# Weights split in pieces of 1024 columns, and a pair's products in another order

## The chip, the cores and the metric

One core of one Trainium2 chip runs the whole program. The metric is the device time of one execution in microseconds. The kernel before takes 1662.88 us (median of three runs, 1662.47 to 1663.27).

## The reference

One inference step of a backbone of one layer for 128 context tokens and 512 latent tokens (640 rows, width 1024): an FFN half step (SwiGLU, inner width 2816), a mixer (a chunkwise mLSTM in both directions beside a gated convolution, merged by gates and projected), a second FFN half step, and a last RMS norm. Each norm is modulated by vectors computed from the condition (adaLN). Cut to what matters here:

```
h = modulate(rmsnorm(x, norm_g[0]), sh1, sc1)
x = x + 0.5 * g1 * swiglu(h, ffn1_w1, ffn1_w2)
h = modulate(rmsnorm(x, norm_g[1]), shm, scm)
z = h @ w_in + b_in            # q, k, v, o, gates, convolution inputs
ml = (o * mlstm(q, k, v, ...)) @ w_ml_out
sc = (bg * conv3(cg * xs)) @ w_sc_out
x = x + gm * ((sigmoid(z_gml) * ml + sigmoid(z_gsc) * sc) @ w_o)
h = modulate(rmsnorm(x, norm_g[2]), sh2, sc2)
x = x + 0.5 * g2 * swiglu(h, ffn2_w1, ffn2_w2)
```

All of it is float32. Nearly all the work is the products of the weights with 640 columns of activations.

## The kernel before

The activations lie transposed, 128 features by 640 tokens, in two halves of 320 columns. A weight block of 128 output features and 1024 inputs is loaded as one tile of 128x1024 (`wr`, five buffers, DMAs on SP's queue).

To reach float32 accuracy with float32r products each operand is split in two: `split` (L74) lets ACT round the tile to float32r (L75, `wh`) and DVE subtract that from the raw tile (L79, `wl`). `three` (L242) then issues three products of 128x128 weights by 320 columns (L245 to L247: high by high, high by low, low by high). A piece of weights that is split at once is here called an op: 512 columns before, so two for a tile; six `wh` and six `wl` buffers, and splitting runs up to four ops ahead (OPB, AHEAD, L82). `cast_more` (L102) issues the splits, in the order in which the ops are used, when an earlier op is taken up by `op()`. `hold` and `release` keep the ops of a stage in their buffers for its second half.

Most of the large products go by pairs (`pair_el`, `pair_steps`, L260): two output blocks against both halves of the columns, as a Strassen-Winograd scheme with seven products instead of eight. A11, A12, A21 and A22 are the quarters of the two weight tiles. S1 = A21 + A22, S2 = S1 - A11, S3 = A11 - A21 and S4 = A12 - S2 are summed on DVE (L218; in ten pairs of the mixer S1 and S3 on POOL). The matching sums of activations (T1 to T4) are ready beforehand. Each of the seven products is four k-blocks by three, so 12 products of 320 columns in a PSUM bank. Partial results are shared between the banks: a gets A11, and ACT copies it into b; b gets S2, and ACT copies that into c (both L273 and L283); b gets S4, c gets S3 and A22, and a gets A12. S1 goes into a bank of its own, which ACT copies out (L279, `p5`).

There are 72 pairs: 38 in the two FFNs, 34 in the mixer. Before, the products stand in the order A11, S1, S2, A12, S3, S4, A22. Each engine works through its own instructions in the order in which the program issues them, with semaphores between engines; there is no scheduler behind it. In each pair other work is woven in: the SwiGLU of the pair before (silu, product, split of `Uh`/`Ul`), sums for the adaLN vectors on DVE (L696), the steps of the mLSTM.

Other stages are plain: `plain_el` (one weight tile by both halves; the second FFN matrix, w_ml_out, w_sc_out, w_o), `halves_el` (the last output blocks before a norm, first all with the first half of the columns, then all with the second, so that the norm can begin), and `head_el` (the first three blocks behind a norm, while the normalised activations are still being split). `first_head` is that for the start of the kernel, where weights, adaLN and activations arrive together; in it nine products of a zero bfloat16 tile (L1110) are issued ahead of the first real ones.

Of the kernel before, what the change touches and what calls it, by code (L numbers as in the profile page):

```python
# [12 lines left out]
P = 128  # L13
# [31 lines left out]
def mixer_step(ctx: ExitStack, tc: tile.TileContext, x_prompt, x_sample, state_C, state_n, state_m,  # L45
# [36 lines left out]
    RAWB, OPB, SB, AHEAD = 5, 6, 4, 4  # L82
    raws, ops = [], []
# [18 lines left out]
    def cast_more(upto):  # L102
        load_more()
        while ptr["cast"] < min(upto, ptr["held"] + OPB, ptr["cap"], len(ops)):
            n = ptr["cast"]
            if not ready(ops[n]):
                return
            while ptr["sum"] < min(n + 2, len(ops)) and ready(ops[ptr["sum"]]):
                o = ops[ptr["sum"]]
                o["ap"] = o["src"](o)  # L110
                ptr["sum"] += 1
            o = ops[n]
            w = o["n"]
# [5 lines left out]
            rdone.update(o["last"])  # L119
            load_more()  # L120
# [87 lines left out]

    LH, RH = slice(0, 512), slice(512, 1024)

    def pair_ops(r1=0, r2=1, e1=None):
        e1 = e1 or V

        def total(key, engine, fn, a, b):
            def src(o):
                g = o["group"].setdefault(r1, {})
                t = g[key] = ring.tile([P, 512], F32, name="ws", bufs=SB)
                getattr(engine, fn)(t, part(o, a), part(o, b))  # L218
                return t
            return src  # L220

        def part(o, key):
            if key[0] == "S":
                return o["group"][r1][key]
            return rtile[o["base"] + (r1 if key[1] == "1" else r2)][:, LH if key[2] == "1" else RH]

        whole = lambda key: lambda o: part(o, key)
        spec = lambda src, *r: {"raws": list(r), "n": 512, "src": src}
        return {
            "A11": spec(whole("A11"), r1), "A12": spec(whole("A12"), r1), "A22": spec(whole("A22"), r2),  # L230
            "S1": spec(total("S1", e1, "tensor_add", "A21", "A22"), r2),
            "S2": spec(total("S2", V, "tensor_sub", "S1", "A11"), r1, r2),
            "S3": spec(total("S3", e1, "tensor_sub", "A11", "A21"), r1, r2),
            "S4": spec(total("S4", V, "tensor_sub", "A12", "S2"), r1, r2),
        }
# [3 lines left out]
    EARLY = ("A11", "A12", "S1", "S2", "S3", "S4", "A22")  # L239
# [20 lines left out]
    def pair_steps(order, ev, spare_v):  # L260
        S = {}

        def prod(name, ps, start):
            hi, lo = op()
            for kk in range(4):
                three(ps[:, :HT], hi, lo, kk, HB[ACT_OF[name]][kk], start and kk == 0, kk == 3)

        for name in order:
            if name == "A11":
# [4 lines left out]
                flush()  # L274
            elif name == "S1":
# [4 lines left out]
            elif name == "S2":  # L280
                prod(name, S["b"], False)
                S["c"] = big()
                A.copy(S["c"][:, :HT], S["b"][:, :HT])  # L283
            elif name == "A12":
                prod(name, S["a"], False)
                ev(0, 0, S["a"][:, :HT])
# [18 lines left out]
    def pair_el(load1, load2, ev, e1=None, spare_v=False):  # L305
        po = pair_ops(e1=e1)

        def emit():
            nf = len(fill)
            for i, _ in enumerate(pair_steps(ORDER, ev, spare_v)):  # L310
                relax(7 - i if i else 9)
                drain(nf - nf * (i + 1) // 7)
        return dict(element([load1, load2], [po[name] for name in ORDER], emit), pair=True)

    def tile_ops(nk, t=0):
        out = []
        for k0 in range(0, nk, 4):
            n = min(4, nk - k0) * P
            out.append({"raws": [0], "n": n,
                        "src": (lambda k0, n: lambda o: rtile[o["base"] + t][:, k0 * P:k0 * P + n])(k0, n)})  # L320
        return out

    def unit(w, nk, acts, h, ev, points=()):
        ps = big()
        for k in range(nk):
            three(ps[:, :HT], *w[k // 4], k % 4, acts(k, h), k == 0, k == nk - 1)
# [9 lines left out]
    def head_el(blocks, chain, work, mid=(), extra=None):  # L336
# [7 lines left out]
        def emit():  # L344
# [20 lines left out]
            w = [[op()] for t in range(3)]  # L365
            ps = [big() for t in range(3)]
            for k in range(KT):
                if k == 4:
                    for t in range(3):
                        w[t].append(op())  # L370
                for t in range(3):
                    three(ps[t][:, :HT], *w[t][k // 4], k % 4, plain_acts(k, 0), k == 0, k == KT - 1)
# [12 lines left out]
            for t in range(3):  # L385
                unit(w[t], KT, plain_acts, 1, ev(t), {3: some, 7: some})
                release(2)
            if extra:
                extra()
            for t in range(3, nb):  # L390
                w = [op(), op()]
# [8 lines left out]
        oa = [dict(tile_ops(KT, at_[t])[i], raws=[at_[t]]) for i in range(2) for t in range(3)]  # L400
        ob = [dict(o, raws=[at_[t]]) for t in range(3, nb) for o in tile_ops(KT, at_[t])]
        el = dict(element(loads, oa + ob, emit), calm=True)
# [5 lines left out]
    def halves_el(loads, nk, acts, ev, after):  # L408

        per = (nk + 3) // 4  # L410

        def emit():
# [4 lines left out]
            for m in range(len(loads)):  # L417
                w = [op() for _ in range(per)]
                ws.append(w)
                unit(w, nk, acts, 0, lambda h, ps, m=m: ev(m, h, ps))  # L420
                squares()
                after(0, m)
            n = 6 // len(loads)
# [5 lines left out]
            for m in range(len(loads)):  # L429
                pts = {nk // 2 - 1: nxt} if n == 2 else {}  # L430

                def done(h, ps, m=m):
# [3 lines left out]
                    else:  # L436
                        ev(m, h, ps)
                        release(per)
                        if m == len(loads) - 1 or n == 2:
# [5 lines left out]
                unit(ws[m], nk, acts, 1, done, pts)  # L445
                if m < 2:
                    release(per)
                    squares()
        return element(loads, [dict(o, raws=[t]) for t in range(len(loads)) for o in tile_ops(nk, t)], emit)

    def plain_el(load, nk, acts, ev, halves=(0, 1)):
        def emit():
            nf = len(fill)
            ps = {h: big() for h in halves}
            w = [op() for _ in range(0, nk, 4)]
            n = 0
            for k in range(nk):
                hi, lo = w[k // 4]
                for h in halves:
                    three(ps[h][:, :HT], hi, lo, k % 4, acts(k, h), k == 0, k == nk - 1)  # L460
                relax(nk - k)
                drain(nf - nf * (k + 1) // nk)
            for h in halves:
                ev(h, ps[h][:, :HT])
            squares()
        return dict(element([load], tile_ops(nk), emit), calm=True)
# [484 lines left out]
    def ffn(w1, w2, g, lists, head_of, e1=None):  # L951

        head, els, f0 = [], [], 0
        for size in GROUPS:
            U = {}
            grp = []
            for j in range(size):
# [17 lines left out]
                else:  # L975
# [4 lines left out]
            w2s = [plain_el(ld(m), size, acts, lambda h, ps, m=m, last=last: add_x(m, h, ps, g, last))  # L980
                   for m in range(KT if not last else 2)]
            w2s[0] = dict(w2s[0], calm=False)
            if last:
                w2s.append(halves_el([ld(m) for m in range(2, KT)], size, acts,
                                     lambda m, h, ps: add_x(m + 2, h, ps, g, True), lists))
# [23 lines left out]
    early = early_x.enter_context(pool("early", side="right"))  # L1009
    for k in range(KT):  # L1010
# [5 lines left out]
    def x_load(ch):  # L1016

        for q in range(2):
            t = XI[ch, q] = ring.tile([P, 512], F32, name=("wh", "wl")[q], bufs=OPB)
# [53 lines left out]
    def first_head(blocks):  # L1073
# [17 lines left out]
        part = lambda t, c: {"raws": [t], "n": 512, "src": lambda o: rtile[o["base"] + t][:, c:c + 512]}  # L1091
# [932 lines left out]
```

## Time and profile before

| | before |
|---|---|
| median of 3 runs | 1662.88 us |
| span of the profiled execution | 1659.7 us |
| TensorE matmul busy | 1642.4 us, 99% |
| TensorE weight load busy | 1601.4 us, 96% |
| DVE busy | 1257.6 us, 76% |
| ACT busy | 791.5 us, 48% |
| POOL busy | 170.7 us, 10% |
| products of `three` (L245 to L247) | 10080 |

The page gives the span of the profiled execution, from its first to its last instruction; no separate time is listed for it. The median of the runs is 3.2 us above it. Products overlap in the array, so the duration of one (0.31 us) is longer than the distance to the next (0.146 us), and it is the distance that counts. A row of a timeline gives start, duration, engine, line, operation, the tile written and the tiles read; in brackets, how long the engine was idle before and on whom it waited.

### The profile page before, as it was taken

How to read it: one execution, taken by the hardware profiler on the slowest of the kernel's cores; microseconds unless marked ns; L12 is line 12 of the kernel's file. 1: busy time of each engine (PE TensorE's matmuls, PEld its weight loads, DVE VectorE, ACT ScalarE, POOL GpSimd, SP SyncE). 2: the span in 40 equal slices, each digit the busy share in tenths (PEclk: the TensorE clock that was granted, in tenths of full speed). 3: DMA queues.
4: the chain of work that ended last, by engine and by line, in shares of the span. 5: the costliest groups of instructions: out<-in, count | busy, mean ns of one | idle time of the engine just before them, and what ended most of it. 6: DMA issues, size and time to landing. Idle time of an engine off the chain costs nothing.

```text
span 1659.7 us, 29315 instructions
## 1 busy us (share of the span) xinstructions
PE 1642.4 (99%) x11201; PEld 1601.4 (96%) x11201; DVE 1257.6 (76%) x2681; ACT 791.5 (48%) x1723; POOL 170.7 (10%) x258
## 2 busy tenths in 40 slices
PE   8999999999999999999999999999999999999998
PEld 5999999999999999999999999999999999999997
DVE  6867877877778878778897898789587467476576
ACT  5642542533566656555561455532375245254253
POOL 2010000000031322111121221011100000000002
PEclk9999999999999999999999999999999999999999
DMA  9454333343352434342367323366241322232222
GB/s 321 115 165 127 111 111 111 102 136 101 108 178 80 113 88 111 75 109 67 96 208 239 106 79 92 101 196 207 90 127 55 99 77 79 74 93 87 77 77 64
DMA packets 273036, 193.08 MB, mean 116 GB/s; under 512 B 7923, under 2 KB 253050, under 8 KB 272896
## 3 DMA queue, kind: packets, MB, share of 16 engines
q1 hardware_dynamic: 263280, 158.36, 32.5%
q0 software_dynamic: 9584, 32.85, 6.8%
q8 instruction: 88, 1.44, 0.4%
q14 instruction: 52, 0.43, 0.1%
q10 hardware_dynamic: 32, 0.01, 0.0%
HBM read 175.87 MB, written 15.31 MB: 115 GB/s over the span
## 4 chain that ended last, share of the span: by engine, by line
PE 91%; DVE 3%; ACT 3%; DMA 2%; issue 1%; SPq 1%; POOL 0%; ACTq 0%; DVEq 0%; POOLq 0%
PE ps L245 28%; PE ps L246 28%; PE ps L247 28%; PE ax L1583 2%; PE ax L1614 2%; DMA wr<-in_ffn_w_dram 1%; PE ax L1586 1%; PE ax L1560 1%; ACT Uh L852 1%; DVE wl L79 0%; ACT wh L75 0%; SPq L552 0%; DVE x L937 0%; DMA wl<-in_x_sample_dram 0%; DVE Uh L844 0%
## 5 line engine op out<-in xcount | busy, mean ns | idle before, releaser
L79 DVE TENSOR_TENSOR wl<-wr,wh 128x512 fp32r<-128x512 f32 (+1 forms) x406 | 265.3, 667 | 79.8 <-ACT wh L75 76.5
L75 ACT CAST wh<-wr 128x512 fp32r<-128x512 f32 (+1 forms) x408 | 237.4, 593 | 158.7 <-PE ps L246 146.1
L79 DVE TENSOR_TENSOR wl<-ws,wh 128x512 fp32r<-128x512 f32 x288 | 203.1, 705 | 44.5 <-ACT wh L75 43.8
L75 ACT CAST wh<-ws 128x512 fp32r<-128x512 f32 x288 | 175.7, 619 | 101.2 <-DVE ws L218 60.0
L245 PE MATMUL ps<-Uh,wh 128*128 128x320 f32 x704 | 218.8, 311 | 0.0
L246 PE MATMUL ps<-Ul,wh 128*128 128x320 f32 x704 | 217.2, 309 | 0.0
L247 PE MATMUL ps<-Uh,wl 128*128 128x320 f32 x704 | 217.2, 308 | 0.0
L937 DVE SCALAR_TENSOR_TENSOR x<-ps,modT,x 128x128 f32<-128x128 f32 (+2 forms) x216 | 82.6, 432 | 114.0 <-PE ps L247 114.0
L245 PEld LDWEIGHTS ps<-Uh,wh 128*128 128x128 f32 x704 | 132.1, 188 | 1.2 <-issue 0.8
L246 PEld LDWEIGHTS ps<-Ul,wh 128*128 128x128 f32 x704 | 132.1, 188 | 0.2 <-DVE Ul L79 0.2
L247 PEld LDWEIGHTS ps<-Uh,wl 128*128 128x128 f32 x704 | 132.1, 188 | 0.0
L245 PE MATMUL ps<-H11h,wh 128*128 128x320 f32 x380 | 120.0, 316 | 0.5 <-ACT H11h L75 0.5
L245 PE MATMUL ps<-HT4h,wh 128*128 128x320 f32 x380 | 119.8, 315 | 0.0
L245 PE MATMUL ps<-H21h,wh 128*128 128x320 f32 x380 | 118.9, 313 | 0.0
L246 PE MATMUL ps<-H11l,wh 128*128 128x320 f32 x380 | 117.7, 310 | 0.3
L246 PE MATMUL ps<-HT4l,wh 128*128 128x320 f32 x380 | 117.5, 309 | 0.1
L247 PE MATMUL ps<-H21h,wl 128*128 128x320 f32 x380 | 117.5, 309 | 0.0
L247 PE MATMUL ps<-HT4h,wl 128*128 128x320 f32 x380 | 117.4, 309 | 0.0
L247 PE MATMUL ps<-H11h,wl 128*128 128x320 f32 x380 | 117.4, 309 | 0.0
L246 PE MATMUL ps<-H21l,wh 128*128 128x320 f32 x380 | 117.2, 308 | 0.0
L245 PE MATMUL ps<-H22h,wh 128*128 128x320 f32 x348 | 108.9, 313 | 0.0
L246 PE MATMUL ps<-H22l,wh 128*128 128x320 f32 x348 | 107.7, 309 | 0.4
(440 smaller groups left out, 4475.6 us busy)
## 6 DMA issues: line engine op xcount, KB each, us to landing
wr<-in_ffn_w_dram SPq DMA_DIRECT2D x86, 512.0 KB, 3.8
wr<-in_w_in_dram SPq DMA_DIRECT2D x72, 512.0 KB, 3.7
wr<-in_w_mod_dram SPq DMA_DIRECT2D x51, 512.0 KB, 3.8
wr<-in_ffn_w_dram SPq DMA_DIRECT2D x48, 384.0 KB, 3.4
early<-in_w_mod_dram SPq DMA_DIRECT2D x13, 512.0 KB, 8.4
wr<-in_ffn_w_dram SPq DMA_DIRECT2D x20, 256.0 KB, 3.2
mg<-in_w_mod_dram POOLq DMA_DIRECT2D x8, 512.0 KB, 5.5
wr<-in_w_ml_out_dram SPq DMA_DIRECT2D x8, 512.0 KB, 4.6
```

Source lines behind the costliest of these rows:

```text
L75: A.copy(hi, raw)
L79: V.tensor_sub(lo, raw, f32(hi))
L245: PE.matmul(ps, hi[:, ws], ah, start=start, stop=False, skip_group_check=True)
L246: PE.matmul(ps, hi[:, ws], al, start=False, stop=False, skip_group_check=True)
L247: PE.matmul(ps, lo[:, ws], ah, start=False, stop=stop, skip_group_check=True)
L852: A.activation(t[:, a:b], t[:, a:b], AF.Identity, scale=sc_, bias=bi_)
L937: V.scalar_tensor_tensor(X[m][:, o + a:o + b], ps[:, a:b], modT[:, g, m, cd:cd + 1], X[m][:, o + a:o + b], op0=OP.mult, op1=OP.add)
L1560: PE.matmul(p[:, :P], S["k", dt][:, sl], S["q", dt][:, sl], start=(dt == 0), stop=(dt == 1))
L1583: PE.matmul(p2[:, :DH + 1], S["q", dt][:, sl], S["C"][d][:, dt, :], start=(dt == 0), stop=(dt == 1))
L1586: PE.matmul(p1[:, :DH + 1], S["p", ch][:, d, :], PO["vt"][:, ch, :], start=True, stop=True)
L1614: PE.matmul(p[:, :DH + 1], kw[:, dt * P:(dt + 1) * P], PO["vt"][:, ch, :], start=True, stop=True)
```

## The change

Weights are now split in ops of 1024 columns: a whole tile in a plain stage (768 or 512 where the FFN's second matrix is cut so), and in a pair four ops: A11 with A12, S1 with S2, S3 with S4, and A22 alone (512). The same memory holds three buffers of twice the size instead of six (two of sums instead of four), and splitting runs two ops ahead. So that the two products of an op follow each other, the seven products of a pair are now A11, A12, S2, S1, S3, S4, A22. In the last group of the FFN's second matrix two output blocks share one tile (`twin_load`, `twin_el`). In the start, ops are cut in two halves that are split apart (`cut`, `defer`), so that the first products still need only 512 columns. The zeros' products become six of 512 columns in float32r, on a tile that POOL clears.

```diff
-    RAWB, OPB, SB, AHEAD = 5, 6, 4, 4
+    RAWB, OPB, SB, AHEAD = 5, 3, 2, 2
...
-            hi = ring.tile([P, 512], F32R, name="wh", bufs=OPB)
-            lo = ring.tile([P, 512], F32R, name="wl", bufs=OPB)
-            split(o["ap"], hi[:, :w], lo[:, :w], ptr.get("owe"))
+            hi = ring.tile([P, 1024], F32R, name="wh", bufs=OPB)
+            lo = ring.tile([P, 1024], F32R, name="wl", bufs=OPB)
+            src, cut = o["ap"], o.get("cut", ((0, o["n"]),))
+            for i, (a, b) in enumerate(cut):
+                part = lambda a=a, b=b: split(src[:, a:b], hi[:, a:b], lo[:, a:b], ptr.get("owe"))
...
+        def s12(t, r1, r2, g):
+            e1.tensor_add(t[:, LH], r2[:, LH], r2[:, RH])
+            V.tensor_sub(t[:, RH], t[:, LH], r1[:, LH])
+
+        def s34(t, r1, r2, g):
+            e1.tensor_sub(t[:, LH], r1[:, LH], r2[:, LH])
+            V.tensor_sub(t[:, RH], r1[:, RH], g["S12"][:, RH])
+        return [{"raws": [0], "n": 1024, "src": lambda o: rtile[o["base"]]},
+                {"raws": [0, 1], "n": 1024, "src": sums("S12", s12)},
+                {"raws": [0, 1], "n": 1024, "src": sums("S34", s34)},
+                {"raws": [1], "n": 512, "src": lambda o: rtile[o["base"] + 1][:, RH]}]
...
-    ORDER = ("A11", "S1", "S2", "A12", "S3", "S4", "A22")
+    ORDER = ("A11", "A12", "S2", "S1", "S3", "S4", "A22")
+    LIES = {"A11": (0, 0), "A12": (0, 4), "S1": (1, 0), "S2": (1, 4), "S3": (2, 0), "S4": (2, 4), "A22": (3, 0)}
...
             if name == "A11":
                 S["a"] = big()
                 prod(name, S["a"], True)
                 S["b"] = big()
                 A.copy(S["b"][:, :HT], S["a"][:, :HT])
                 flush()
+            elif name == "A12":
+                prod(name, S["a"], False)
+                ev(0, 0, S["a"][:, :HT])
+            elif name == "S2":
+                prod(name, S["b"], False)
+                S["c"] = big()
+                A.copy(S["c"][:, :HT], S["b"][:, :HT])
             elif name == "S1":
                 e = big()
                 prod(name, e, True)
                 S["p5"] = t3()
                 A.copy(S["p5"], e[:, :HT])
...
+    def twin_el(load, nk, acts, ev):
+        def emit():
+            w = op()
+            for i in range(2):
+                ps = [big(), big()]
+                for k in range(nk):
+                    for h in (0, 1):
+                        three(ps[h][:, :HT], *w, nk * i + k, acts(k, h), k == 0, k == nk - 1)
...
-            for i in range(9):
-                PE.matmul(z[:, :HT], zero[:, :P], zero, start=True, stop=True)
+            for i in range(6):
+                PE.matmul(z, wide0[:, :P], wide0, start=True, stop=True)
```

How the order moves is shown at three places of one pair in the second FFN. In the rows, `ps` is a PSUM bank, `wh` and `wl` the split weights, `H11h`, `H21h` and `HT1h` the split activations that A11, A12 and S1 multiply, `ws` the sums of weights; the numbers tell buffers apart, and `waits` names the engines whose semaphores an instruction waits for. In the changed kernel `three` stands at L261 to L263, the copies into b and c at L291 and L299, that of `p5` at L304.

TensorE where A11 ends and the next product begins, before:

```order
L246 MATMUL ps_16724<-H11l_14803,wh_16641 128x320
L247 MATMUL ps_16724<-H11h_14802,wl_16642 128x320
L245 MATMUL ps_16747<-HT1h_15096,wh_16661 128x320 [waits DVE_49,Activation_49]
L246 MATMUL ps_16747<-HT1l_15097,wh_16661 128x320
L247 MATMUL ps_16747<-HT1h_15096,wl_16662 128x320
```

and changed:

```order
L262 MATMUL ps_15582<-H11l_13801,wh_15522 128x320
L263 MATMUL ps_15582<-H11h_13800,wl_15523 128x320
L261 MATMUL ps_15582<-H21h_13808,wh_15522 128x320 [waits Activation_49]
L262 MATMUL ps_15582<-H21l_13809,wh_15522 128x320
L263 MATMUL ps_15582<-H21h_13808,wl_15523 128x320
```

A11 is followed by A12 in the same bank and with the same weight tile, where S1 followed in another bank with another tile.

ACT up to the copy from a into b, from the silu of the pair before on, before:

```order
L963 ACTIVATE t3_16696<-t3_16617 128x320 [waits DVE_49]
L75 CAST Uh_16698<-t3_16508 128x320
L75 CAST wh_16704<-wr_16333 128x512 [waits PE_49,Activation_49]
L75 CAST Uh_16720<-t3_16547 128x320
L75 CAST wh_16727<-ws_16702 128x512 [waits DVE_49,PE_49,Activation_49]
L273 COPY ps_16743<-ps_16724 128x320 [waits PE_49,Activation_49]
```

and changed:

```order
L988 ACTIVATE t3_15418<-t3_15382 128x320 [waits DVE_49]
L75 CAST Uh_15420<-t3_15220 128x320
L75 CAST wh_15427<-ws_15384 128x1024 [waits PE_49,Activation_49]
L75 CAST Uh_15443<-t3_15291 128x320
L75 CAST wh_15448<-ws_15424 128x1024 [waits DVE_49,PE_49,Activation_49]
L291 COPY ps_15466<-ps_15447 128x320 [waits PE_49,Activation_49]
```

The copy stands behind the split of a sum in both; it was S1's, of 512 columns, and is now that of S3 with S4, of 1024.

DVE from the sum that follows S4 on, before:

```order
L297 TENSOR_TENSOR t3_16766<-ps_16743,t3_16766 128x320 [waits DVE_49,PE_49]
L79 TENSOR_TENSOR Ul_16848<-t3_16657,Uh_16847 128x320 [waits Activation_49]
L218 TENSOR_TENSOR ws_16851<-wr_16474,wr_16603 128x512
L79 TENSOR_TENSOR wl_16854<-wr_16474,wh_16853 128x512 [waits Activation_49]
L79 TENSOR_TENSOR Ul_16870<-t3_16696,Uh_16869 128x320 [waits Activation_49]
```

and changed:

```order
L315 TENSOR_TENSOR t3_15652<-ps_15601,t3_15652 128x320 [waits DVE_49,PE_49]
L79 TENSOR_TENSOR Ul_15691<-t3_15482,Uh_15690 128x320 [waits Activation_49]
L246 TENSOR_TENSOR ws_15694<-wr_15353,wr_15452 128x512
L247 TENSOR_TENSOR ws_15694<-wr_15353,ws_15654 128x512
L79 TENSOR_TENSOR wl_15698<-ws_15654,wh_15697 128x1024 [waits Activation_49]
L79 TENSOR_TENSOR Ul_15714<-t3_15553,Uh_15713 128x320 [waits Activation_49]
```

One sum stood behind the first `Ul` (S1's); now two do (S3's and S4's), and the subtraction behind them covers 1024 columns.

More of the change, by code (lines that the diff above doesn't have):

```diff
@@ L228, in pair_ops @@
[L228 to L235, printed above, removed]
+                t = o["group"][key] = ring.tile([P, 1024], F32, name="ws", bufs=SB)
@@ L406, in blocks_of, with halves_el @@
         return [(p[i], lambda h, ps, i=i: p[2](i, h, ps)) for i in range(2)]
[L408 to L410 removed]
+    def halves_el(loads, nk, acts, ev, after, two=False):
+        nb = len(loads) * (1 + two)
         def emit():
@@ L416, in emit @@
             ws = []
[L417 to L420, printed above, removed]
+            for m in range(nb):
+                if not two or m % 2 == 0:
+                    ws.append(op())
+                unit(ws[-1], nk, acts, 0, lambda h, ps, m=m: ev(m, h, ps), k0=nk * (m % 2) if two else 0)
                 squares()
                 after(0, m)
-            n = 6 // len(loads)
+            n = 6 // nb
             at_ = {"i": 0}
@@ L428, in nxt, with free @@
                 at_["i"] += 1
-            for m in range(len(loads)):
+            def free(m):
+                if not two or m % 2:
+                    release(1)
+            for m in range(nb):
                 pts = {nk // 2 - 1: nxt} if n == 2 else {}
@@ L1009, in mixer_step @@
     early = early_x.enter_context(pool("early", side="right"))
+    wide0 = early.tile([P, 512], F32R, name="wide0")
+    G.memset(f32(wide0), 0.0)
     for k in range(KT):
```

172 lines of the change are left out of this document (85 added, 87 removed).

## The prediction

> **What bounds the kernel now.** I read the engines' totals first, then the clock, then one 100 us stage, then the waits of TensorE.
>
> ```profile
> PE 1642.4 (99%) x11201; PEld 1601.4 (96%) x11201; DVE 1257.6 (76%) x2681; ACT 791.5 (48%) x1723; POOL 170.7 (10%) x258
> PEclk9999999999999999999999999999999999999999
> ...
> 500.00:600.00 100.00, 100.00 (x703) 97.17 (x702) 78.28 (x166) 64.11 (x147) 26.34 (x45) 1.00 0.41 105
> ...
> 1400.00:1500.00 100.00, 100.00 (x685) 100.00 (x683) 61.12 (x119) 38.88 (x82) 0.00 (x0) 1.00 0.29 85
> ...
> PE ps L245 <- ACT ps L273: 0.4, 1, 0.4
> ```
>
> TensorE sets the time: 99% busy at an undisturbed clock, 685 products of 320 columns in 100 us of an FFN stage, so one starts every 0.146 us. (The two stage rows give length, busy time and count for PE, weight loads, DVE, ACT, POOL, then the granted clock.) The last row is one of only a few waits of TensorE on another engine: a wait on the PSUM copies of a pair (L273), once, 0.4 us. So fewer or larger instructions on ACT and DVE are worth nothing by themselves; the question is whether TensorE meets a new wait.
>
> **What the change costs, step 1: a wait that was covered.** After product A11, ACT copies the accumulator a into b. Before, S1 follows A11 and goes into a fresh bank; A12, which accumulates onto a, comes two products later. Now A12 follows A11 directly and writes the bank that ACT still has to read. The new order shows the wait on ACT at A12's first product, and neither operand explains it: the weight tile was already used by A11, the activations are old. So TensorE must drain A11, let ACT copy, and go on. It cannot pass to S2, which stands behind A12 in its queue. That happens once per pair, and the pairs are counted here:
>
> ```profile
> L273 ACT COPY ps<-ps x72: 410/410/429, 79.8 to 1604.8; 128x320 f32<-128x320 f32 x72
> ```
>
> What a stop of that kind costs is seen once in the trace, in two places of the same pair. ACT had been late there, so S2 had to wait for the same copy:
>
> ```profile
> 77.82 0.31 PE L247 MATMUL ps<-H11h,wl 128*128 128x320 f32 x1
> ...
> 79.58 0.30 PE L247 MATMUL ps<-HT1h,wl 128*128 128x320 f32 x1
> 79.80 0.41 ACT L273 COPY ps<-ps 128x320 f32<-128x320 f32 x1
> 80.26 0.19 PEld L245 LDWEIGHTS ps<-HT2h,wh 128*128 128x128 f32 x1 [0.63 <-ACT ps L273]
> 80.26 0.41 PE L245 MATMUL ps<-HT2h,wh 128*128 128x320 f32 x1 [0.38 <-ACT ps L273]
> 80.52 0.31 PE L246 MATMUL ps<-HT2l,wh 128*128 128x320 f32 x1
> ```
>
> The copy ends at 80.21; TensorE starts 0.05 later, and its second product comes after 0.26 instead of 0.146, since the weight load that is otherwise hidden has also waited: 0.11 more. An undisturbed copy starts 0.40 after A11's last product (1475.97 to 1476.37 in the next fence). So the **floor** per pair is 0.40 + 0.41 + 0.05 - 0.146 + 0.11 = 0.82 us, and 72 x 0.82 = 59 us.
>
> **Step 2: ACT is often not free then.** ACT takes its instructions in order, and in the new order the last one before the copy is the split of S3 and S4, now one cast of 1024 columns, which needs two sums from DVE. Here is an FFN pair of before; A22 starts at 1472.60, which I call 0, and A11 at 1474.36, or 1.76 (12 products):
>
> ```profile
> 1472.60 0.31 PE L245 MATMUL ps<-HT4h,wh 128*128 128x320 f32 x1
> 1475.97 0.31 PE L247 MATMUL ps<-H11h,wl 128*128 128x320 f32 x1
> ...
> 1473.33 0.47 ACT L963 ACTIVATE t<-t 128x320 f32<-128x320 f32 x1 [2.58 <-DVE t L297]
> 1473.70 0.44 ACT L75 CAST Uh<-t 128x320 fp32r<-128x320 f32 x1
> 1474.05 0.61 ACT L75 CAST wh<-wr 128x512 fp32r<-128x512 f32 x1
> 1474.57 0.46 ACT L75 CAST Uh<-t 128x320 fp32r<-128x320 f32 x1
> 1475.38 0.62 ACT L75 CAST wh<-ws 128x512 fp32r<-128x512 f32 x1 [0.36 <-DVE ws L218]
> 1476.37 0.41 ACT L273 COPY ps<-ps 128x320 f32<-128x320 f32 x1 [0.37 <-PE ps L247]
> ...
> 1472.80 0.49 DVE L297 TENSOR_TENSOR t<-ps,t 128x320 f32<-128x320 f32 x1 [0.67 <-PE ps L247]
> 1474.18 0.49 DVE L79 TENSOR_TENSOR Ul<-t,Uh 128x320 fp32r<-128x320 f32 x1 [0.89 <-ACT Uh L75]
> 1474.59 0.68 DVE L218 TENSOR_TENSOR ws<-wr 128x512 f32<-128x512 f32 x1
> 1475.19 0.68 DVE L79 TENSOR_TENSOR wl<-wr,wh 128x512 fp32r<-128x512 f32 x1
> ...
> L75 ACT CAST wh<-wr 128x512 fp32r<-128x512 f32 x360 | 219.4, 618 | 126.6 <-PE ps L246 114.1 <-DMA wr<-in_w_ml_out_dram 4.8 <-DMA wr<-in_ffn_w_dram 4.5
> L75 ACT CAST wh<-wr 128x256 fp32r<-128x256 f32 x48 | 19.4, 405 | 32.0 <-PE ps L246 32.0
> ```
>
> The chain up to DVE's Ul is the same in both kernels: 0.20 L297, 0.73 silu, 1.10 Uh, 1.58 Ul. In the changed order two sums of 512 columns follow Ul: 1.99, and 0.60 later 2.59, done at 3.27. Those two must both be done before the S3/S4 cast, which starts about 0.1 later, at 3.38 (that gap is 1475.38 against a sum that began at 1474.59 and took 0.68). A cast costs 213 ns per 256 columns by the last two rows, so 1024 take 1.04 us, and the next instruction can start after 0.52 + 0.43 = 0.95 (1474.05 to 1474.57 for 512, plus 512 columns). The copy therefore starts at 4.33, where A11 would have allowed 3.77, and ends at 4.74; A12 starts at 4.79 instead of 3.52. With the 0.11 that is **1.38 us**. The chain starts anew from each S4, so the next pair does not absorb it.
>
> By the order of the changed kernel, 18 of the 72 pairs have exactly this form. In 5 of FFN1 a piece of the adaLN sums stands between Ul and the two sums as well:
>
> ```profile
> 341.30 0.75 DVE L696 SCALAR_TENSOR_TENSOR ma<-wr,cm,ma 128x512 f32<-128x512 f32 x1
> 341.96 0.69 DVE L218 TENSOR_TENSOR ws<-wr 128x512 f32<-128x512 f32 x1
> ```
>
> That is 0.66 more, 2.04. In 23 pairs no Ul stands there (first pairs of a group, most pairs of the convolution and the gates): the sums come early and the floor holds. Six others (one behind the w_ml_out stage, five near the convolution) lie between, 1.2 each. In 17 pairs beside the mLSTM steps ACT and DVE also carry that work. There the copy of before was on time in some pairs and late in others, as here:
>
> ```profile
> 627.74 0.31 PE L247 MATMUL ps<-H11h,wl 128*128 128x320 f32 x1
> 628.31 0.62 ACT L75 CAST wh<-ws 128x512 fp32r<-128x512 f32 x1
> 628.83 0.42 ACT L273 COPY ps<-ps 128x320 f32<-128x320 f32 x1
> ```
>
> 1.09 instead of 0.40 after the last product, by a cast that will be 0.43 longer and wait for a second sum: 0.82 to 2.5, and I take 1.3, nearer the floor. The 3 pairs behind the heads start with ACT in arrears, as at 77.82, where the copy came 1.98 after the last product: (1.98 + 0.41 + 0.05 - 0.15 + 0.11) plus 0.43 for the longer cast, 2.8.
>
> Sum: 18 x 1.38 = 24.8; 5 x 2.04 = 10.2; 23 x 0.82 = 18.9; 6 x 1.2 = 7.2; 17 x 1.3 = 22.1; 3 x 2.8 = 8.4. Together **92 us**.
>
> **Step 3: the rest.** About 350 merged casts and as many subtractions each save ACT 0.09 us (0.52 less 0.43 of columns) and DVE about 0.07 us. Both have idle time throughout, TensorE waits for neither, so this counts as nothing; were DVE the bound, it would be some 25 us. Weights arrive in fewer, larger steps: the three whole tiles of a head are wanted at once, and the third buffer comes free only when the stage before has ended. A cast of 1.04 and a subtraction of about 1.2 (0.68 for 512 in the rows above, of which the next could start after 0.60) stand against 9 products, 1.3 us: about 1.5 us at each of two heads, between 0 and 4; I take 3 together. The weight transfers keep size and order, on SP's queue. The zeros' products run on TensorE while it waits for ACT:
>
> ```profile
> 19.49 1.39 PE L1110 MATMUL ps<-nrow 128*128 128x320 bf16 x9
> 21.40 0.41 PE L245 MATMUL ps<-H11h,wh 128*128 128x320 f32 x1 [0.52 <-ACT H11h L75]
> ```
>
> Six of 512 columns, at 0.146 x 512/320 = 0.234 each, take 1.41 us against nine at about 0.139, 1.25. The gap of 0.52 hides that; uncovered it is 0.2 us. Its memset on POOL comes after POOL's last constant load, where nothing else waits for POOL.
>
> The Trainium skill speaks against this change in Perfetto Trace Analysis, section Optimizing Scalar/DVE Operations: larger operations pay where the engine is saturated, and where ACT or DVE is not saturated but causes bubbles on another engine, instructions should rather be broken up. By that page and the sum above, casts left at 512 columns would let the 18 pairs come nearer the floor, some 8 us less; no run shown here tells.
>
> **Total.** 1659.7 span plus 92 plus 3 is 1755. The runs' median of 1662.9 is 3.2 above the span, which is start and end around it and does not change: **1757 us**, 5.7% slower.
>
> **Rivals.**
> *Only the floor.* If ACT is free at every copy (DVE gains from its merged work and the sums come earlier), 72 x 0.82 = 59: 1722 to 1725 us. For it: ACT is only 48% busy. Against: the chain above runs from S4's end, not from a backlog. 0.14.
> *More.* Mixer pairs at 2.5, pairs behind heads at 5, heads at 4: 92 + 20 + 7 + 8 = 127, 1790 us and above. For it: beside the mLSTM ACT is up to 64% busy, with work in between that waits in its turn. A form of it is a clock that falls in the new gaps. The trace holds 1.00 across gaps of 0.6 us in the start; if half clock covered a tenth of the span, 10080 products x 0.146 us / 10 would be 147 us more, but stops of 1 to 2 us in 13 are still 90% busy. 0.11 for both.
> The Trainium skill, TensorE: Matmul & The Clock Gate, Part 1, lets the clock fall only after an idle window of about 3.4 us, which none of the estimated stops reaches; no run here shows that limit.
> *No change.* The wait at A12 is on something long done (a cast), and TensorE is not held: 1661 to 1665 us. This needs ACT's copy to be out of the condition, which a later write to the same bank speaks against. 0.03.
> *Not slower: faster.* TensorE starts products a little late where it met other work, and in the first 50 us it idles while weights and activations are split:
>
> ```profile
> 0.00:50.00 50.00, 42.63 (x307) 30.37 (x308) 34.37 (x123) 27.25 (x67) 10.57 (x26) 1.00 1.06 318
> ```
>
> Of 50 us, 7.4 are idle. If fewer splits took half of it and A12's wait were hidden, 1659 us. It decides only if the copy ended within 0.15 us of A11's last product, and the copy alone takes 0.41. 0.03.
>
> **How the numbers follow.** My case has 0.69; its own range is 1735 to 1780. Stretched to the floor and to the "more" case, the 8-in-10 range is 1720 to 1790. A difference under 0.2% cannot be told from none here (three runs spread over 0.05%). Slower has 0.69 + 0.14 + 0.11 = 0.94, same 0.03, faster 0.03.
>
> **What would show it.** Right: TensorE's share falls from 99% to about 94%; a wait of TensorE on the pair's copy appears 72 times, 0.7 to 2 us each; inside FFN pairs A12 starts about 1.4 us late and a pair takes 13.7 us instead of 12.3; the pace inside products stays 0.146. DVE's share falls to about 71%. Wrong: no such wait (step 1), waits of 0.8 everywhere (step 2), a granted clock below 1 (the clock), or the gain or loss lying in the first 50 us or at the heads (step 3).

## The result and the profile after

The changed kernel takes **1776.8 us** (median of four runs, 1774.5 to 1782.2) against 1663.1 us of the kernel before beside it: 1.0691 times as long, 95% interval 1.0679 to 1.0703. The forecast was 1757 us with a range of 1720 to 1790: the side and the place were right, the sum was 20 us short.

The page of the profile after, as before: span, busy time of the engines, and the granted clock in 40 slices.

```profile
span 1780.4 us, 28579 instructions
PE 1683.1 (95%) x11198; PEld 1619.6 (91%) x11198; DVE 1234.7 (69%) x2372; ACT 753.5 (42%) x1414; POOL 173.2 (10%) x259
PEclk9999999999989999999999999999999999999999
```

The waits of TensorE on other engines (in all, how often, the longest):

```profile
PE ps L261 <- ACT ps L291: 68.1, 70, 2.8
PE ps L261 <- ACT wh L75: 7.1, 2, 4.2
PE ps L261 <- DVE t L312: 1.9, 2, 1.1
```

And two stages of 100 us, read like the stage rows in the prediction (the last three numbers are clock, DMA share and GB/s):

```profile
500.00:600.00 100.00, 92.42 (x635) 86.51 (x635) 71.61 (x148) 58.37 (x119) 14.57 (x25) 0.95 0.36 108
1400.00:1500.00 100.00, 95.57 (x645) 94.25 (x644) 57.66 (x91) 33.84 (x55) 0.00 (x0) 1.00 0.26 76
```

The wait on the copy of bank a, which was seen once before, now stands 70 times in the list. In the FFN stage (the second row) 100 us hold 645 products instead of 685, at the full clock. In the stage around the mixer's head (the first row) the mean granted clock falls to 0.95 besides. DVE and ACT have less to do than before (1234.7 us busy instead of 1257.6, and 753.5 instead of 791.5), and the time does not fall for it.

One FFN pair of the timeline after, ACT first, then TensorE where A11 ends:

```profile
1473.14 0.47 ACT L988 ACTIVATE t<-t 128x320 f32<-128x320 f32 x1 [2.67 <-DVE t L315]
1473.52 0.44 ACT L75 CAST Uh<-t 128x320 fp32r<-128x320 f32 x1
1473.87 1.04 ACT L75 CAST wh<-ws 128x1024 fp32r<-128x1024 f32 x1
1474.81 0.46 ACT L75 CAST Uh<-t 128x320 fp32r<-128x320 f32 x1
1475.80 1.05 ACT L75 CAST wh<-ws 128x1024 fp32r<-128x1024 f32 x1 [0.53 <-DVE ws L247]
1476.75 0.42 ACT L291 COPY ps<-ps 128x320 f32<-128x320 f32 x1
...
1475.79 0.31 PE L263 MATMUL ps<-H11h,wl 128*128 128x320 f32 x1
1477.22 0.41 PE L261 MATMUL ps<-H21h,wh 128*128 128x320 f32 x1 [1.12 <-ACT ps L291]
1477.47 0.31 PE L262 MATMUL ps<-H21l,wh 128*128 128x320 f32 x1
...
1489.50 0.31 PE L263 MATMUL ps<-H11h,wl 128*128 128x320 f32 x1
```

The last row is the last product of the next pair's A11. The A11 of this pair ends with the product at 1475.79. At that moment ACT is just starting the 1024-column cast for S3/S4, which had waited for DVE's second sum (L247). The copy gets its turn at 1476.75 and is done at 1477.17, and A12 starts 0.05 later. From A11's last product to A12's second 1.68 us pass where 0.29 would: a stop of 1.39.

**Where the 120.7 us between the two profiled spans went.** The usual distance from one product to the next is 0.1466 us. From the starts of all TensorE products I took, for the products of `three` at the full clock, what each distance clearly exceeds that. Before, these excesses sum to 26.2 us, after to 131.5. Of the 105.3 more, A12's first two products hold 86.7 (79.5 and 7.2), the two heads about 9, and some 10 are scattered; what causes those 10 was not traced. Products that ran at half clock, 0.267 us apart, cost another 13.6, and the small products outside `three` 1.1. Together 120.0.

### The profile page after: what moved, and what is told of

Its sections match the earlier page's. It is cut to its first block, busy times and chain, and to the rows that moved or that the text cites. A ratio compares the mean times of both kernels' runs of the same rounds, so it can differ in the third digit from the quotient of the medians.

```text
span 1780.4 us, 28579 instructions
## 1 busy us (share of the span) xinstructions
PE 1683.1 (95%) x11198; PEld 1619.6 (91%) x11198; DVE 1234.7 (69%) x2372; ACT 753.5 (42%) x1414; POOL 173.2 (10%) x259
## 4 chain that ended last, share of the span: by engine, by line
PE 50%; DVE 7%; ACT 5%; issue 3%; DMA 0%; ACTq 0%; DVEq 0%
PE ps L261 16%; PE ps L262 15%; PE ps L263 15%; ACT wh L75 2%; PE ax L1615 1%; PE ax L1646 1%; DVE wl L79 1%; ACT ps L291 1%; DVE t L315 1%; DVE ws L247 1%; PE ax L1618 1%; DVE ws L246 1%; DVE Ul L79 0%; ACT Uh L75 0%; PE ax L1592 0%
## 5 line engine op out<-in xcount | busy, mean ns | idle before, releaser
L79 DVE TENSOR_TENSOR wl<-wr,wh 128x512 fp32r<-128x512 f32 (+2 forms) x241 | 244.5, 1015 | 222.6 <-ACT wh L75 218.2
L75 ACT CAST wh<-wr 128x512 fp32r<-128x512 f32 (+2 forms) x243 | 210.3, 866 | 174.3 <-PE ps L262 157.6
L261 PE MATMUL ps<-Uh,wh 128*128 128x320 f32 x704 | 218.9, 311 | 0.3 <-ACT Uh L75 0.3
L263 PE MATMUL ps<-Uh,wl 128*128 128x320 f32 x704 | 217.1, 308 | 0.0
L79 DVE TENSOR_TENSOR wl<-ws,wh 128x1024 fp32r<-128x1024 f32 x144 | 183.6, 1278 | 19.7 <-ACT wh L75 19.5
L261 PE MATMUL ps<-H21h,wh 128*128 128x320 f32 x380 | 126.9, 334 | 69.1 <-ACT ps L291 68.1
L75 ACT CAST wh<-ws 128x1024 fp32r<-128x1024 f32 x144 | 149.6, 1045 | 95.2 <-PE ps L262 54.5
L261 PEld LDWEIGHTS ps<-H21h,wh 128*128 128x128 f32 x380 | 72.3, 190 | 87.9 <-ACT ps L291 86.5
L261 PEld LDWEIGHTS ps<-Uh,wh 128*128 128x128 f32 x704 | 132.1, 188 | 1.9 <-issue 1.2
L263 PEld LDWEIGHTS ps<-Uh,wl 128*128 128x128 f32 x704 | 132.1, 188 | 0.0
L261 PE MATMUL ps<-H11h,wh 128*128 128x320 f32 x380 | 123.3, 325 | 7.5 <-ACT wh L75 7.1
L261 PE MATMUL ps<-HT4h,wh 128*128 128x320 f32 x380 | 119.8, 315 | 1.9 <-DVE t L312 1.9
L263 PE MATMUL ps<-H11h,wl 128*128 128x320 f32 x380 | 120.3, 317 | 1.1 <-DVE wl L79 1.1
L263 PE MATMUL ps<-H21h,wl 128*128 128x320 f32 x380 | 119.5, 314 | 0.0
L263 PE MATMUL ps<-HT4h,wl 128*128 128x320 f32 x380 | 117.6, 309 | 0.0
L261 PE MATMUL ps<-H22h,wh 128*128 128x320 f32 x348 | 108.8, 313 | 0.0
```

Of the source, the lines that this page charges most:

```text
L75: A.copy(hi, raw)
L79: V.tensor_sub(lo, raw, f32(hi))
L261: PE.matmul(ps, hi[:, ws], ah, start=start, stop=False, skip_group_check=True)
L263: PE.matmul(ps, lo[:, ws], ah, start=False, stop=stop, skip_group_check=True)
```

## The experiments

All of them are timed beside the kernel before, so ratios to it are given. "Half clock" is the time that the trace's clock record shows at 0.50, without the last microseconds of the kernel, where it falls in every run, before too.

**1. The old order with long pieces.** Only the order goes back. Since A11 and A12 share one split piece, its buffer is kept while S1 and S2 run.

```diff
-    ORDER = ("A11", "A12", "S2", "S1", "S3", "S4", "A22")
+    ORDER = ("A11", "S1", "S2", "A12", "S3", "S4", "A22")
...
-            ptr["held"] = n
+            ptr["held"] = n - keep
...
-                W.append(op())
+                W.append(op(1 if n == 1 else 0))
```

> The changed kernel with the products of a pair in the order of before (A11, S1, S2, A12, S3, S4, A22); pieces of 1024 columns, buffers, start and zeros' products stay changed. Theory (TensorE waits at A12 for ACT's copy out of its own bank): the 70 waits on that copy and their 68 us vanish, and the clock drops inside pairs with them; what is left over the kernel before is the two heads, about 9 us of waits plus some 5 of slow clock behind them: 1668 to 1682 us. Rival (pieces of 1024 columns are late by themselves, whatever the order): most of the 114 us stays, over 1740.

Measured: **1784.5 us**, ratio 1.0734 [1.0718, 1.0750]. The theory missed by over 100 us. The wait on the copy is gone, but the waits of TensorE show two others in its place:

```profile
PE ps L261 <- DVE t L312: 46.0, 46, 1.6
PE ps L263 <- DVE wl L79: 23.2, 38, 2.8
```

DVE's timeline in one pair shows why (in brackets, idle time ahead):

```profile
301.02 0.69 DVE L79 TENSOR_TENSOR wl<-wr,wh 128x512 fp32r<-128x512 f32 x1 [4.36 <-ACT wh L75]
301.63 0.68 DVE L242 TENSOR_TENSOR ws<-wr 128x512 f32<-128x512 f32 x1
302.35 0.69 DVE L243 TENSOR_TENSOR ws<-ws,wr 128x512 f32<-128x512 f32 x1
302.96 1.22 DVE L79 TENSOR_TENSOR wl<-wr,wh 128x1024 fp32r<-128x1024 f32 x1
304.09 0.48 DVE L312 TENSOR_TENSOR t<-ps,t 128x320 f32<-128x320 f32 x1
```

L312 reads bank c after S3, and A22 can only accumulate into c when it is done. DVE idles for 4.36 us and then does two subtractions of splits and two sums, 3.1 us, in front of L312. The splits come so late because the edit keeps a buffer, and the program issues a split only when it has a buffer free for it; experiment 6, which issues the splits elsewhere, bears that out. So this run tells that the old order cannot take over the changed kernel's splitting as it stands. It does not tell whether pieces of 1024 can be fed at all in the old order. Experiments 6 to 8 ask that.

**2. The new order with the old pieces.** The kernel before, with its 512-column pieces, in the order of the change; S1 is summed just ahead of S2, which needs it.

```diff
-    ORDER = ("A11", "S1", "S2", "A12", "S3", "S4", "A22")
+    ORDER = ("A11", "A12", "S2", "S1", "S3", "S4", "A22")
```

> The kernel before with only the new order of products (A11, A12, S2, S1, S3, S4, A22); pieces of 512 columns, six buffers. S1 and S2 are summed one after the other, since S2 is now needed first. Theory: 72 waits at A12, each at least 0.82 us, few much longer since the cast ahead of the copy has 512 columns: 59 to 80 us, 1722 to 1745, clock at least 0.997, heads as before. Rival (1024 columns are the cause): within 5 us of 1663.

Measured: **1729.1 us**, ratio 1.0399 [1.0383, 1.0414].

```profile
PE ps L250 <- ACT ps L278: 46.2, 70, 2.1
```

The order alone brings the 70 waits. A12's first two products lose 62.6 us here, against 83.3 in the changed kernel; the median stop is the floor, 0.82. (Both sums go over 68 pairs, without the four in which small products of the mLSTM stand between A11 and A12.) So the old pieces save 21 us of stops. In the 18 pairs for which the prediction estimated some 8 us less, the stops fall from 25.1 to 14.9 us, 10 less. The Trainium skill's advice in Perfetto Trace Analysis, section Optimizing Scalar/DVE Operations, that breaking instructions up may help where they cause bubbles on another engine, agrees with the sign. But this run takes back the six buffers and the splitting four pieces ahead together with the short pieces, so it does not show the share of the short casts alone.

**3. The copy ahead of the split.** The changed kernel; while A11 is issued, the splits that follow are held back and issued behind the copy.

```diff
-                W.append(op())
+                W.append(op(0 if name == "A11" else AHEAD))
...
                 A.copy(S["b"][:, :HT], S["a"][:, :HT])
+                cast_more(ptr["use"] + AHEAD)
```

> The changed kernel with ACT's copy from a into b issued ahead of the split of S3 with S4 instead of behind it; order of products and pieces stay changed. Theory: the wait at A12 stays but falls to its floor, 0.82 us, in nearly all FFN pairs (1.39 and 2.06 in the changed kernel): 72 x 0.82 = 59, a few us more beside the mLSTM, and no clock drops inside the FFN pairs; with the heads' 9 to 14 us 1730 to 1745. Rival (the wait is not held by what stands ahead of the copy on ACT): no change, 1770 to 1780.

Measured: **1747.3 us**, ratio 1.0511 [1.0494, 1.0529].

```profile
PE ps L261 <- ACT ps L291: 40.3, 70, 1.4
```

The same 70 waits cost 28 us less, although no instruction became shorter. A12's loss at 68 pairs falls from 83.3 to 57.6 us, 0.85 each: the floor. So step 2 of the prediction (the copy queues behind the long cast) is shown, and its size is 26 us. The time is 2 us above the expected range. That had 9 to 14 us for the heads, whose waits are as they were, 7.1 us in all, and 20.5 us at half clock around them; and it had nothing for scattered excesses like the 10 us above, which this run has too, about 9 us by the starts of the products.

**4. A longer stop.** The changed kernel, with two more copies of bank a on ACT into a tile that nobody reads, ahead of the real one.

```diff
+                pad = tp.tile([P, HT], F32, name="pad")
+                for _ in range(2):
+                    A.copy(pad, S["a"][:, :HT])
```

> The changed kernel with two further copies of the same bank into an unused tile ahead of ACT's copy from a into b, about 0.7 us of ACT; nothing reads them. It measures the granted clock, which in the changed kernel fell to half for 3.4 us or a multiple nine times, six of them right behind a stop of 2 us or more. If stops of about 2 us bring it about: the 0.82 stops become 1.5, the 1.39 ones 2.1, the 2.06 ones 2.8; 72 x 0.7 = 50 us by the stops and many more drops, clock 0.95 to 0.98, 1840 to 1890 us. If the drops have another cause (the heads, chance): clock 0.99, 1825 to 1830.

Measured: **1851.2 us**, ratio 1.1134 [1.1112, 1.1157].

```profile
PE ps L261 <- ACT ps L294: 123.0, 71, 3.5
```

```profile
core 0: 1850.5 us, clock 0.977
```

The first row is again the wait at A12, the second the mean granted clock. The stops at 68 pairs grow by 53 us, but the span by 70. The time at half clock grows from 41 to 78.5 us, and its cost from 13.6 to 27.6. Longer stops cost more than their own length, as the theory of the clock said.

**5. TensorE kept busy during the stops.** The changed kernel, with bf16 products of zeros in TensorE's way: five ahead of each A12 (into the bank that S1 overwrites), eighteen ahead of the third block's first product in the two heads.

```diff
+    def busy(ps, n):
+        for i in range(n):
+            PE.matmul(ps[:, :HT], zfill[:, :P], zfill, start=True, stop=True)
...
             elif name == "A12":
+                S["e"] = big()
+                busy(S["e"], 5)
                 prod(name, S["a"], False)
...
+                    if k == 0 and t == 2:
+                        busy(ps[2], 18)
                     three(ps[t][:, :HT], *w[t], k, plain_acts(k, 0), k == 0, k == KT - 1)
```

> The changed kernel with bf16 products of zeros put into TensorE's stops: five of 320 columns ahead of each A12 (into the bank that S1 overwrites later), eighteen ahead of the third block's first product of the two heads (into a bank that this product overwrites). They shorten no wait for the copy. Theory, the clock falls because TensorE idles for more than about 0.6 of a 3.4 us window: the time at half clock falls from 41 us to under 12, and the time by 12 to 20 us, to 1757 to 1765. Rival, the clock falls for another reason than idle time (load, or a fixed pattern), or zeros do not count: 1772 or more, with some 40 us at half clock; if the zeros themselves stand in the way, above 1777.

Measured: **1768.3 us** (1765.0 to 1768.6), ratio 1.0630 [1.0612, 1.0647].

```profile
PE ps L261 <- ACT ps L295: 24.5, 34, 2.1
```

```profile
core 0: 1766.8 us, clock 0.997
```

The time at half clock falls from 41 to 6.8 us, as expected, and its cost from 13.6 to 2.2 us. The kernel gains 8.6 us, 3 less than the bottom of what was expected. That time lies between the ranges of the two theories and does not decide between them; the time at half clock does, for the rival expected some 40 us of it. The copy comes no sooner than before, and yet more work on TensorE made the kernel faster. So the slow clock came from the idle time.

**6. The old order again, splits spread.** As experiment 1, but A22's and the next A11/A12's splits are issued behind L312, the next pair's sums earlier, the S3/S4 split behind the first copy.

```diff
-                W.append(op(1 if n == 1 else 0))
+                W.append(op(1 if n == 1 else 0, AHEAD if n == 3 else 0))
...
                 A.copy(S["b"][:, :HT], S["a"][:, :HT])
                 flush()
+                cast_more(ptr["use"] + AHEAD)
...
                 ev(0, 0, S["a"][:, :HT])
+                sum_more(ptr["use"] + 4)
...
                     V.tensor_add(S["c22"], S["c"][:, :HT], S["p5"])
+                cast_more(ptr["use"] + AHEAD)
```

> The changed kernel (pieces of 1024 columns, three buffers) with the old order A11, S1, S2, A12, S3, S4, A22, and the splits and sums spread: A22's and the next A11/A12's splits are issued behind VectorE's sum of the S3 product instead of ahead of it, the next pair's sums ahead of S3, the S3/S4 split behind the first copy. In the first run of the old order VectorE stood idle 4.0 to 4.4 us of a pair and then did 3.3 us of splitting ahead of that sum, for which A22 waited 46 times. Theory 1, the order alone forced the stops and the pieces only lengthen what a short cover meets: the stops of the pairs go, the two heads with about 9 us and some 6 to 10 us of slow clock stay, 1672 to 1692 us. Theory 2, pieces of 1024 in three buffers cannot be fed in the old order, so that the new order was needed for them: still over 1730 us, with TensorE waiting for splits or for VectorE at A22 or S1 in most pairs.

Measured: **1730.7 us**, ratio 1.0409 [1.0393, 1.0424], which is by its number just on theory 2's side. But the wait at A22 is gone, and of the two that had taken over one is left:

```profile
PE ps L269 <- DVE wl L79: 19.3, 44, 1.0
```

S1's third product waits for the low half of its piece. That split's cast stood on ACT behind an eviction, and it came about 0.5 us too late in 50 of the 72 pairs, 26 us by the starts of the products.

**7. That split earlier.** As experiment 6, with the next pair's S1/S2 split issued right behind DVE's sum after S4.

```diff
                 V.tensor_add(S["p5"], S["b"][:, :HT], S["p5"])
+                ptr["held"] += 1
+                cast_more(ptr["use"] + 3)
```

> The run before (old order, pieces of 1024, splits spread) with the next pair's S1/S2 split issued right behind VectorE's sum of the S4 product, ahead of the eviction of that sum. There the cast of this split stood on ScalarE behind an eviction (L997) and a cast of Uh, ended 2.9 us after S4's last product, and S1's third product waited 0.4 us for the low half in 50 pairs, 31 us in all. Theory 1, the order alone forced the stops of the change, and pieces of 1024 can be fed without stops in the old order: these 50 waits go, and the heads (9 us) and the slow clock behind them (10 to 20 us at half, half of that lost) stay: 1672 to 1700 us. Theory 2, splits of 1024 do not fit into three buffers whatever is done: the waits come back elsewhere, over 1720 us.

Measured: **1694.8 us**, ratio 1.0196 [1.0181, 1.0211], in theory 1's range.

```profile
PE ps L267 <- ACT wh L75: 7.1, 2, 4.2
PE ax L1702 <- DVE hs L1693: 2.0, 1, 2.0
PE ps L269 <- DVE wl L79: 1.9, 4, 0.7
```

```profile
300.00:325.60 25.60, 25.60 (x177) 25.60 (x176) 20.99 (x34) 13.04 (x23) 0.00 (x0) 1.00 0.35 103
```

Of that wait 1.9 us in four places are left. In the second fence, a stretch of FFN pairs, TensorE has no pause: 177 products in 25.6 us, one each 0.145. The top row of the waits is the two heads. Set beside the kernel before, product by product, the run stays within 0.7 us of it through all of the first FFN, and the distance stays the same to 0.3 us through the pairs of the second; its 33 us more of span are all lost in between, in the mixer and the two heads. So pieces of 1024 columns in three buffers can be fed in the old order, and they cost the FFN pairs nothing. The new order was one way to suit them, not the only one. Whether they cost the mixer's pairs something stays open.

**8. The heads.** As experiment 7; in the two heads the third block's products lag the other two blocks' by four steps of the contraction.

```diff
+            LAG = 4
-            for k in range(KT):
+            for k in range(KT + LAG):
                 for t in range(3):
-                    three(ps[t][:, :HT], *w[t], k, plain_acts(k, 0), k == 0, k == KT - 1)
+                    kt = k - LAG * (t == 2)
+                    if 0 <= kt < KT:
+                        three(ps[t][:, :HT], *w[t], kt, plain_acts(kt, 0), kt == 0, kt == KT - 1)
```

> The same, and in the two heads the third block's products lag the other two blocks' by four steps of the contraction (24 products, 3.5 us), so that the third piece, whose buffer the last pair's A22 frees only when that pair ends, has that much longer. Theory 1: the heads' waits of 4.2 and 2.9 us and the slow clock behind them go too, and nothing is left of the loss: 1658 to 1670 us. Theory 2, or a wait in the heads that is not the third piece's: within 5 us of the run without the lag.

Measured: **1684.1 us**, ratio 1.0133 [1.0116, 1.0150]: 10.7 us less, where 25 or more were expected. The list of waits has no head any more:

```profile
PE ax L1705 <- DVE hs L1696: 2.0, 1, 2.0
PE ax L875 <- DVE dg L868: 1.9, 2, 1.0
```

So the heads' wait was the third piece's, and it was worth about 11 us with the clock behind it. Some 22 us stay over the kernel before, all of them lost between the end of the first FFN and the pairs of the second. By the starts of the products, 8.5 of them are short excesses in `three` beside the mLSTM and the convolution, 1.9 slow clock, and 11.1 are small products (transposes, the norms' sums, mLSTM steps), which wait for DVE and ACT a little longer in many places. Whether that comes from longer instructions on those engines, from fewer buffers or from the spread order was not tried. No version here beats the kernel before.

**9. The zeros' products alone.** The kernel before with six float32r products of 512 columns in place of nine bf16 ones.

```diff
-            for i in range(9):
-                PE.matmul(z[:, :HT], zero[:, :P], zero, start=True, stop=True)
+            for i in range(6):
+                PE.matmul(z, wide0[:, :P], wide0, start=True, stop=True)
```

> The kernel before with only the products of zeros changed: six float32r ones of 512 columns in place of nine bf16 ones of 320. Theory: nothing, 1661 to 1665 us, since the two traces agree again by product 240. Rival: they warm the clock later or hold the first products, 1 to 3 us slower.

Measured: **1662.4 us**, ratio 1.0001 [0.9991, 1.0010]. No difference, as predicted.

## Why the prediction was right, and where it was short

**Step 1, the wait that was covered: right.** The floor was given as 0.82 us per pair. Many pairs without other work stop for 0.77 to 0.82 us, and with the copy put first (experiment 3) the mean is 0.85. The order alone costs 66 us by experiment 2's median, of which 59 were the predicted floor of 72 pairs.

**Step 2, the copy in ACT's queue: right.** For the FFN pair it predicted 1.38 us and a stop of 1.39 is measured; exactly 18 pairs stop for 1.38 to 1.40. With a piece of the adaLN sums it predicted 2.04 for five pairs; 2.06 is measured four times, 1.79 once. Pairs beside the mLSTM stop for 0.8 to 3.0. The three pairs behind the heads were put at 2.8 each and stop for 2.59, 1.45 and 0.82. The whole term was 92 us and is 87. The FFN pair takes 13.7 us, as it said (A11's last product at 1475.79, that of the next pair at 1489.5), TensorE's share is 95% where 94% was forecast, and DVE's 69% where 71% was.

**Step 3, the heads: mis-sized.** It took 1.5 us for each, 3 together; they cost 5.0 and 3.9, where it gave 0 to 4 to each. This is the mixer's head:

```profile
512.22 0.31 PE L263 MATMUL ps<-H11h,wl 128*128 128x320 f32 x1
...
515.25 0.44 ACT L75 CAST H21h<-Ul 128x320 fp32r<-128x320 f32 x1
515.60 1.04 ACT L75 CAST wh<-wr 128x1024 fp32r<-128x1024 f32 x1
...
516.69 0.64 PE L261 MATMUL ps<-H11h,wh 128*128 128x320 f32 x1 [4.16 <-ACT wh L75]
...
517.95 0.63 PE L263 MATMUL ps<-H11h,wl 128*128 128x320 f32 x1 [0.36 <-DVE wl L79]
```

The step counted the cast and the subtraction of the third piece, as if ACT began them when the buffer came free. It did not count what stands ahead of them on ACT: the norm chain and the splits of the normalised activations. The cast starts 3.4 us after the last product that TensorE could do. (The small term for the zeros' products took 0.139 us for each of the old ones; their starts are 0.136 apart. Experiment 9 shows that the term is nothing either way.)

**The clock: dismissed, and wrong.** The prediction put a falling clock into a rival of 0.11 because its gaps seemed too short. Nine times the clock fell to half, 41 us in all. In the profiled run that cost 13.6 us, about half of what the sum lacked there. Here are a stop of 2.06 us, which began at 209.1, and one of 2.96 us, which began at 759.2, each with two stretches of 3.4 us around it:

```profile
209.07 0.31 PE L263 MATMUL ps<-H11h,wl 128*128 128x320 f32 x1
211.17 0.42 PE L261 MATMUL ps<-H21h,wh 128*128 128x320 f32 x1 [1.79 <-ACT ps L291]
...
208.20:211.60 3.40, 1.61 (x12) 1.35 (x11) 3.40 (x6) 1.72 (x3) 0.00 (x0) 1.00 0.24 28
211.60:215.00 3.40, 3.40 (x15) 3.40 (x15) 2.17 (x4) 0.58 (x2) 0.00 (x0) 0.50 0.78 255
...
759.21 0.31 PE L263 MATMUL ps<-H11h,wl 128*128 128x320 f32 x1
762.20 0.42 PE L261 MATMUL ps<-H21h,wh 128*128 128x320 f32 x1 [2.68 <-ACT ps L291]
...
757.70:761.10 3.40, 1.82 (x13) 1.55 (x11) 3.26 (x8) 1.71 (x4) 1.00 (x2) 1.00 0.70 105
761.10:764.50 3.40, 2.30 (x16) 2.29 (x17) 3.16 (x8) 2.19 (x5) 0.67 (x1) 1.00 0.59 158
```

The first stretch holds the whole first stop, and in the next one TensorE runs at 0.50, 15 products instead of 23. The second stop is longer, but it falls across the border at 761.1, so that each stretch holds only a part of it, and the clock stays. The Trainium skill's rule that the prediction quoted (TensorE: Matmul & The Clock Gate, Part 1, a fall after an idle window of about 3.4 us) has the length right, but its condition is stricter than what is measured: the falls at 81.9, 211.6, 242.3 and 368.6 us followed stops of 2.06 to 2.59 us.

**The rest.** The range held the time, and so did the narrower one of the prediction's own case, 1735 to 1780. The median lies near the top of that, 3 us below its end, and the slowest of the four runs is above it: the 20 us that were missing come from terms that the prediction put at 3 us or at nothing, and A12's five too many made up for a part of them. The upper rival ("more") had the right ingredients, the heads and the clock, with the wrong sizes. Terms against the trace: A12 92 to 87, heads 3 to 9, clock 0 to 13.6, scattered excesses 0 to 10, small products 0 to 1.

## What to carry to other kernels

When an order of products is changed, look for the product that covered a read of its neighbour's PSUM bank: its absence costs the drain, the copy and the restart, here 0.82 us, once for every pair. A short instruction that TensorE waits for should be issued ahead of long ones on its engine; that was worth 29 us here without making anything shorter (in the profiled runs the stops shrank by 26 us, and the time at half clock was halved). And longer pieces in fewer buffers were fed here only once the splits were placed around the instructions that free banks and buffers (1784.5 us without that, 1694.8 with it), so where the splits are issued has to be planned anew with them.

## What the hardware showed that was not expected

**The clock falls on a fixed grid of 3.413 us.** In the nine kernels with falls, every fall of one run begins and ends on one grid with a step of 3.4133 us, to within 2 ns, and lasts one to three steps of it. The grid's place differs from run to run. Call a step of the grid a window. For each window I summed the time in which TensorE started nothing (what distances over 0.25 us exceed 0.147). Of the 4476 windows at full clock:

| idle share of the window | windows | followed by half clock |
|---|---|---|
| under 0.55 | 4421 | 1 |
| 0.55 to 0.60 | 10 | 3 |
| 0.60 and more | 45 | 43 |

So in these runs it took about 2 us of idle time in one window, with one exception at a share of 0.39: experiment 1, at 576.8 us, where the window also holds 14 products of only 2 or 20 columns. Whether such products count as idle time is not shown. A stop of 1.4 us stays below that; one of 2 us costs up to 1.7 us more (half of a window), if it falls inside one, which is chance. That probably also spreads the changed kernel's runs over 0.4%, where the kernel before spread over 0.05%: the slowest of them has a mean granted clock of 0.987, the fastest 0.992.

**The restart.** Behind each wait the second product came 0.25 us after the first instead of 0.146 (1477.22 to 1477.47 above), in 68 pairs 7 us in all.
